# Rounded and low part of x as one moving operand of 512 columns in a hybrid-layer kernel

## Chip, cores and metric

The kernel runs on one core of one Trainium2 chip. The metric is device time in microseconds, the median of several executions. Engines in the profile: PE (TensorE), PEld (its weight loads), DVE (VectorE), ACT (ScalarE), POOL (GpSimd) and SP (the queue that issues most loads).

## The reference, cut to what matters

One layer with four branches over x (256 tokens x 2048 features, fp32), all fed by one wide projection, and merged by gates.

```python
h = einsum('bsd,de->bse', x, w_in) + b_in          # 2048 -> 18048 columns
(a_x, a_gate, q, k, v, b_gate, c_r, c_k, c_v, c_wd, c_ad, c_gate,
 d_val, d_glu, d_gate, merge_logits) = split(h, ...)
y_a = gated linear recurrence over a causal convolution of a_x
y_b = attention of q, k, v in three groups, 4 heads each
y_c = RWKV-7 recurrence over shifted c_r, c_k, c_v, c_wd, c_ad
y_d = silu(layernorm(31-tap depthwise conv(d_val * sigmoid(d_glu))))
merge_g = sigmoid(merge_logits)                    # 4 x 2048 columns
mixed = sum_n merge_g[n] * ((y_n * silu(gate_n)) @ w_br[n])
out = layernorm(ALPHA * x + mixed @ w_out) * ln_g + ln_b
```

## The kernel before

**Precision.** Matmuls of the large products take fp32r operands. Each fp32 operand is split into a rounded part (h) and what is left (l), and a product is three matmuls: h with rounded x, h with low x, l with rounded x. x is split once, by `split_x`, into `xh` and `xl`, each 128 partitions x 16 row blocks x 256 tokens. Weights are split as they arrive: `split` (L202) loads a chunk (two row blocks x 512 columns, 512 KB) to `raw` over SP's queue, ScalarE casts it to `wh` (L208), DVE subtracts to get `wl`. There are four buffers of `raw`, three of `wh`, three of `wl`. DVE's instructions all carry L65, the helper that issues them.

**Two forms of product.** `channel_major` (matmuls in `multiply`, L229) holds weights and moves x: out are 128 channels x 256 tokens per column tile; two tiles share a PSUM bank, so 512 columns take two banks. `token_major` (L279) holds x and moves 512 weight columns; 256 tokens take two banks. Both loop over eight chunks of weights; in channel-major the four column tiles are the loop inside a chunk, then its two row blocks, then the three matmuls. Both take banks from `pss` (four banks). Side work takes banks from `psb` (four).

**Order.** The main stream is: `opening` (a_x and d_glu), d_val, c_r, the 128 columns c_wd and c_ad (`cwa`), c_k, c_v, gate A, merge of A, gate D, merge of D, gate C, queries, keys, values, gate B, merge of C, merge of B, output product, layernorm. After each chunk, `pump(BUD)` lets the generators in `side` (parameter loads, `lru`, `conformer`, `rwkv`, `attention`) issue work worth a budget of 1300 ns; they run one after another. DVE work of `side` keeps its program order. A scheduler then sets a fixed order on each engine from a model of times; the two instructions of a weight split are raised in priority by `AHEAD`.

**Leaving PSUM.** `biased` and `head_tiles` (L887, L936) empty a channel-major plane by one ScalarE instruction (identity with bias). `silu_gate` (L299) uses one ScalarE sigmoid and one DVE instruction that adds the bias to the plane and multiplies.

**Buffers.** `tt` gives planes of 128 x 4 x 256 fp32 out of five, `rk` out of twelve, `ra` 512 columns out of six. `merge` loads a bias row block for each 512 columns over GpSimd's queue into `bm` (two buffers, L842). That queue also carries the recurrent branch's trips through DRAM (`scr`, `al`, `xt`, `x11`). At the end `shift` takes three banks of `psb` for each half of the tokens.

Of the kernel before, what the change touches and what calls it, by code (L numbers as in the profile page):

```python
# [19 lines left out]
P = 128  # L20
# [53 lines left out]
def tile_hybrid(  # L74
# [8 lines left out]
    ap = ctx.enter_context(tc.tile_pool(name="ap", bufs=1))  # L83
    wp = ctx.enter_context(tc.tile_pool(name="wp", bufs=1))
    xp = ctx.enter_context(tc.tile_pool(name="xp", bufs=1))
    bp = ctx.enter_context(tc.tile_pool(name="bp", bufs=1))
    pss = ctx.enter_context(tc.tile_pool(name="pss", bufs=4, space=PSUM))
    psb = ctx.enter_context(tc.tile_pool(name="psb", bufs=4, space=PSUM))
    dp = ctx.enter_context(tc.tile_pool(name="dp", bufs=1, space=DRAM))

    def big(tag, bufs, name, dt=F32):
        pool = ap if tag in ("mx4", "tt") else xp if tag in ("yh", "yl") else bp
        return pool.tile([P, NJ, T], dt, tag=tag, name=name, bufs=bufs)

    def tt(name, dt=F32):
        return big("tt", 5, name, dt)

    def rk(name, dt=F32):
        return big("rk", 12, name, dt)
# [11 lines left out]
    for _ in range(9):  # L111
        PE.matmul(idle, zero[:, 0:P], zero, start=True, stop=True)

    xh = xp.tile([P, KT, T], F32R, tag="xh", name="xh")
    xl = xp.tile([P, KT, T], F32R, tag="xl", name="xl")
    xr = x_t.rearrange("(k p) t -> p k t", p=P)

    def load_x(k, n):
# [10 lines left out]
    sums = cp.tile([P, CS_X0 - CS_BLK], F32R, name="sums")  # L129
    pkt = cp.tile([P, NJ, N_PK], F32, name="pkt")  # L130
    mut = cp.tile([P, 13], F32, name="mut")
    upt = cp.tile([P, BW], F32, name="upt")
    bd = []

    def load(t, src):
        tc.keep_in_program_order(nc.sync.dma_start(t, src))

    def load_parameters():
        for _ in range(5):
            yield pause()  # L140
        load(bc, b_col)
        load(mut, mu)
        yield pause()
        load(pkt, pk)
        yield pause()
        load(upt, w_up)
        yield pause()
        load(cs, cst[:, 0:CS_BLK])
        t = rk("sums_f").rearrange("p a b -> p (a b)")[:, 0 : CS_X0 - CS_BLK]
        load(t, cst[:, CS_BLK:CS_X0])  # L150
        V.tensor_copy(sums, t)
        yield pause()
        blocks = rk("blocks")
        V.memset(blocks, 0.0)
        bd.extend((blocks[:, :, 0:P], blocks[:, :, P:T]))
        for t, src in zip(bd, (gate_a, gate_x)):
            s4 = src.rearrange("(j e) i o -> i j e o", e=2)
            load(t[0:64, :, 0:64], s4[:, :, 0, :])
            load(t[64:128, :, 64:128], s4[:, :, 1, :])
            yield pause()  # L160
# [38 lines left out]
        pump(1e12)  # L199


    def split(src, c0, n, k, nk, queue=None):  # L202
        raw = wp.tile([P, nk, n], F32, tag="raw", name="raw", bufs=4)
        (queue or nc.sync).dma_start(raw, src[:, k : k + nk, c0 : c0 + n])
        h = wp.tile([P, nk, n], F32R, tag="wh", name="wh", bufs=3)
        l = wp.tile([P, nk, n], F32R, tag="wl", name="wl", bufs=3)
        with tc.high_priority(offset=AHEAD):
            S.copy(h, raw)  # L208
            V.tensor_tensor(l, raw, h.bitcast(F32), op=ALU.subtract)
        return h, l  # L210
# [27 lines left out]
    def channel_major(src, nk, c0, n, rh, rl, budget):  # L238
        ps = columns(n)
        for k0, kn in pieces(nk, n):  # L240
            multiply(ps, *split(src, c0, n, k0, kn), k0, kn, nk, rh, rl)
            pump(budget * n * kn / (512 * KP))
        return ps

    def opening(cols, budget):

# [45 lines left out]
        return channel_major(w_in_r, KT, c0, n, xh, xl, BUD)  # L292

    def silu_gate(c0, name):
        ps = proj(c0)
        g = tt(name)
        for j in range(NJ):
            b = bcol(c0 + j * P)
            S.activation(g[:, j, :], ps[j], AF.Sigmoid, bias=b)  # L299
            V.scalar_tensor_tensor(g[:, j, :], ps[j], b, g[:, j, :], op0=ALU.add, op1=ALU.mult)  # L300
        return g

    def gated(y, g, name):
# [34 lines left out]
    def lru(ax, sps, res):  # L338
        (sp8,) = sps
        u = tt("u")  # L340
        for j in range(NJ):
            V.tensor_scalar(u[:, j, :], ax[:, j, :], col(PK_CONV + 3, j), col(PK_CONVB, j), op0=ALU.mult, op1=ALU.add)
            for back in range(1, 4):
                o = u[:, j, back:T]
                V.scalar_tensor_tensor(o, ax[:, j, 0 : T - back], col(PK_CONV + 3 - back, j), o, op0=ALU.mult, op1=ALU.add)
            yield 1300
        th = tt("th")
        gi = tt("gi")
        for j in range(NJ):
            ps = bank("psg")  # L350
            PE.matmul(ps[:, 0:T], bd[0][:, j, :], u[:, j, :], start=True, stop=True)
            PE.matmul(ps[:, T:], bd[1][:, j, :], u[:, j, :], start=False, stop=True, skip_group_check=True)
            S.activation(th[:, j, :], ps[:, 0:T], AF.Sigmoid, bias=col(PK_GAB, j))
            S.activation(gi[:, j, :], ps[:, T:], AF.Sigmoid, bias=col(PK_GXB, j))
            yield 0
        rd = tt("rd")
        rs = tt("rs")
        for j in range(NJ):
            V.tensor_scalar(th[:, j, :], th[:, j, :], sp8[:, j : j + 1], None, op0=ALU.mult)
        yield 800  # L360
        S.activation(rd, th, AF.Exp, scale=-1.0)
        S.activation(th, th, AF.Tanh, scale=0.5)
        V.tensor_scalar(rd, rd, 0.5, 0.5, op0=ALU.mult, op1=ALU.add)
        V.scalar_tensor_tensor(rs, th, 1.0, rd, op0=ALU.add, op1=ALU.mult)
        yield 1700
        V.scalar_tensor_tensor(rd, rs, 2.0, rd, op0=ALU.subtract, op1=ALU.mult)
        yield 1100
        V.tensor_scalar(rs, th, 1e-33, None, op0=ALU.max)
        S.activation(rs, rs, AF.Sqrt)
        V.tensor_tensor(u, gi, u, op=ALU.mult)  # L370
        yield 1700
        V.scalar_tensor_tensor(th, th, 1e17, rs, op0=ALU.mult, op1=ALU.min)
        yield 1100
        V.scalar_tensor_tensor(th, th, -2.0, rd, op0=ALU.mult, op1=ALU.mult)
        yield 1100
        V.tensor_tensor(u, u, th, op=ALU.mult)
        yield 1100
        V.tensor_scalar(rd, rd, -2.0, -1.0, op0=ALU.mult, op1=ALU.add)
        yield 600
        y = gi  # L380
        for j in range(NJ):
            V.tensor_tensor_scan(y[:, j, :], rd[:, j, :], u[:, j, :], 0.0, ALU.mult, ALU.add)
        yield 1400
        res.append(y)
# [13 lines left out]
    def conformer(cu, res):  # L398
# [8 lines left out]
                    )  # L407
                yield 400
        ps = bank("psm")
        total(ps, parts(acc, tt))  # L410
        mean = bp.tile([P, T], F32, tag="s1", name="mean", bufs=4)
        S.activation(mean, ps[:, 0:T], AF.Copy, scale=1.0 / BW)
        V.tensor_tensor(acc, acc, mean[:, None, :].to_broadcast([P, NJ, T]), op=ALU.subtract)
        sq = tt("csq")
        S.activation(sq, acc, AF.Square)
        yield 1100
        ps = bank("psv")
        total(ps, parts(sq, tt))
        rstd = bp.tile([P, T], F32, tag="s1", name="rstd", bufs=4)
        S.activation(rstd, ps[:, 0:T], AF.Sqrt, bias=eps_ln, scale=1.0 / BW)  # L420
        V.reciprocal(rstd, rstd)
# [61 lines left out]
    def rwkv(craw, cwa, res):  # L483
# [18 lines left out]
        yield 700  # L502
        sg = rk("sg")
        a = rk("a")
        for j in range(NJ):
            ps = bank("pswa")
            PE.matmul(ps[:, 0:T], upt[0:64, j * P : (j + 1) * P], wa[0:64], start=True, stop=True)
            S.activation(sg[:, j, :], ps[:, 0:T], AF.Sigmoid, bias=col(PK_W0, j))
            ps = bank("pswa")
            PE.matmul(ps[:, 0:T], upt[64:128, j * P : (j + 1) * P], wa[64:128], start=True, stop=True)  # L510
            S.activation(a[:, j, :], ps[:, 0:T], AF.Sigmoid, bias=col(PK_A0, j))
            yield 0
# [325 lines left out]
    def merge(n, yh, yl, first, last):  # L838
        for c in range(4):
            c0 = C_M + n * DM + c * 512  # L840
            bias = bp.tile([P, 512], F32, tag="bm", name="bm", bufs=2)
            G.dma_start(bias, row(b_row[c0 : c0 + 512]))  # L842
            ps = token_major(w_in_r, KT, c0, *by_token(xh, xl), BUD)
            gs = []
# [3 lines left out]
                S.activation(g, g, AF.Sigmoid)  # L848
                gs.append(g)
            if last and c == 3:  # L850
                mhl.extend(xp.tile([P, KT, T], F32R, tag="x" + q, name="m" + q) for q in "hl")
                side.extend(channels(i) for i in range(3))
            pb = token_major(w_br_r[:, n * NJ : (n + 1) * NJ, :], NJ, c * 512, *by_token(yh, yl), BUD)
            for t in range(2):
# [33 lines left out]
        return t  # L888

    def shifted(c0, name):  # L890
        return biased(rk(name), c0, proj(c0))

    ya, yb, yc, yd = [], [], [], []
    cu = pad_tile("cu")
# [11 lines left out]

    craw = [shifted(C_R, "cr")]
    cwa = bp.tile([P, T], F32, tag="s1", name="cwa", bufs=4)
    ps = proj(C_WA, 128)
    S.activation(cwa, ps[0], AF.Identity, bias=bcol(C_WA))  # L910
    craw += [shifted(C_CK, "ck"), shifted(C_CV, "cv")]
    side.append(rwkv(craw, cwa, yc))

# [16 lines left out]
    def head_tiles(c0, name):  # L930
        r = []
        for g in range(3):
            t = rk(name)
            ps = proj(c0 + g * 512)
            for j in range(NJ):
                S.activation(t[:, j, :], ps[j], AF.Identity, bias=bcol(c0 + g * 512 + j * P))  # L936
            r.append(t)
        return r

    qt = head_tiles(C_Q, "qt")  # L940
# [17 lines left out]
    merge(1, *yhb, False, True)  # L958


    z = [[tt("z").rearrange("p a b -> p (a b)") for _ in range(2)] for _ in range(2)]
    for t in range(2):
        for i in range(2):
            G.dma_start(z[t][i], x[t * P : (t + 1) * P, i * 1024 : (i + 1) * 1024])
# [182 lines left out]
```

## Time and profile before

| | |
|---|---|
| time, median of 3 runs | 1057.73 us (1057.43 to 1058.16) |
| profiled execution, own time | 1057.35 us |
| its span | 1055.6 us |
| granted TensorE clock, mean | 0.995 of full |
| PEld busy | 921.2 us, 87% |
| ACT busy | 497.0 us, 47% |
| DMA queue of SP and ACT | 185.16 MB, 58.9% of 16 engines' span |

The span runs from the first to the last instruction; the table has what the rows below leave out. Busy time of PE counts matmuls whose ends are modelled and which overlap, so it is an upper figure. "idle <- X" names what ended the idle time before an instruction.

### The profile page before, as it was taken

How to read it: one execution, taken by the hardware profiler on the slowest of the kernel's cores; microseconds unless marked ns; L12 is line 12 of the kernel's file. 1: busy time of each engine (PE TensorE's matmuls, PEld its weight loads, DVE VectorE, ACT ScalarE, POOL GpSimd, SP SyncE). 2: the span in 40 equal slices, each digit the busy share in tenths (PEclk: the TensorE clock that was granted, in tenths of full speed). 3: DMA queues.
4: the chain of work that ended last, by engine and by line, in shares of the span. 5: the costliest groups of instructions: out<-in, count | busy, mean ns of one | idle time of the engine just before them, and what ended most of it. 6: DMA issues, size and time to landing. Idle time of an engine off the chain costs nothing.

```text
span 1055.6 us, 16618 instructions
## 1 busy us (share of the span) xinstructions
PE 1042.8 (99%) x6669; PEld 921.2 (87%) x6669; DVE 722.2 (68%) x985; ACT 497.0 (47%) x594; POOL 41.4 (4%) x75
## 2 busy tenths in 40 slices
PE   7999999999999999999999999999999999999997
PEld 6999999887789877899999998898888888888886
DVE  5769988999969996665544444556666565556656
ACT  3365445557734435434544443346565444345341
POOL 0010000000020020000100000000000000000000
PEclk9999999999999999999999999999999999999998
DMA  8885766665686677555866666664556667676662
GB/s 279 247 254 155 204 187 186 189 183 150 186 215 187 199 206 200 182 154 151 288 180 181 182 187 189 194 183 142 170 154 209 209 202 206 207 226 199 193 192 89
DMA packets 108174, 203.11 MB, mean 192 GB/s; under 512 B 8436, under 2 KB 17296, under 8 KB 108096
## 3 DMA queue, kind: packets, MB, share of 16 engines
q1 hardware_dynamic: 102160, 185.16, 58.9%
q0 software_dynamic: 4928, 15.30, 5.0%
q10 hardware_dynamic: 1008, 1.57, 0.4%
q8 instruction: 52, 0.85, 0.3%
q14 instruction: 26, 0.21, 0.1%
HBM read 198.98 MB, written 5.39 MB: 194 GB/s over the span
## 4 chain that ended last, share of the span: by engine, by line
PE 93%; DVE 3%; DMA 2%; issue 1%; ACT 0%; SPq 0%; DVEq 0%; POOL 0%
PE ps L279 50%; PE ps L229 36%; DVE xw L65 1%; DVE wl L65 1%; PE ps L1056 1%; DMA raw<-in_w_in 1%; DMA x<-scr 1%; PE psl L803 1%; DMA xt<-scr 1%; DVE z L65 0%; PE po L827 0%; PE pab L580 0%; PE pm L872 0%; PE py L736 0%; PE pu L699 0%
## 5 line engine op out<-in xcount | busy, mean ns | idle before, releaser
L65 DVE TENSOR_TENSOR wl<-raw,wh 128x1024 fp32r<-128x1024 f32 (+1 forms) x345 | 417.7, 1213 | 275.5 <-ACT wh L208 274.2
L208 ACT CAST wh<-raw 128x1024 fp32r<-128x1024 f32 (+1 forms) x345 | 358.9, 1043 | 470.4 <-PE ps L279 240.7
L229 PE MATMUL ps<-xh,wh 128*128 128x256 f32 x1040 | 295.2, 285 | 4.3 <-ACT wh L208 4.3
L229 PE MATMUL ps<-xl,wh 128*128 128x256 f32 x1040 | 294.1, 284 | 0.0
L229 PE MATMUL ps<-xh,wl 128*128 128x256 f32 x1040 | 291.7, 285 | 0.0
L279 PE MATMUL ps<-wh,xh 128*128 128x512 f32 x608 | 237.9, 391 | 0.0
L279 PE MATMUL ps<-wh,xl 128*128 128x512 f32 x608 | 237.2, 390 | 0.0
L279 PE MATMUL ps<-wl,xh 128*128 128x512 f32 x608 | 221.0, 393 | 0.5 <-DVE wl L65 0.5
L229 PEld LDWEIGHTS ps<-xh,wh 128*128 128x128 f32 x1040 | 199.1, 191 | 5.8 <-ACT wh L208 4.5
L229 PEld LDWEIGHTS ps<-xl,wh 128*128 128x128 f32 x1040 | 199.1, 191 | 0.3
L229 PEld LDWEIGHTS ps<-xh,wl 128*128 128x128 f32 x1040 | 196.9, 191 | 0.7 <-DVE wl L65 0.2
L279 PEld LDWEIGHTS ps<-wl,xh 128*128 128x128 f32 x608 | 114.1, 188 | 26.4 <-DVE wl L65 1.6
L279 PEld LDWEIGHTS ps<-wh,xl 128*128 128x128 f32 x608 | 114.1, 188 | 23.9 <-issue 0.3
L279 PEld LDWEIGHTS ps<-wh,xh 128*128 128x128 f32 x608 | 114.2, 188 | 23.2 <-ACT wh L208 0.3
L65 DVE SCALAR_TENSOR_TENSOR acc<-cu,pkt,acc 128x256 f32<-128x256 f32 x120 | 50.7, 481 | 0.0
L279 PE MATMUL ps<-wh,ml 128*128 128x512 f32 (+1 forms) x128 | 46.5, 364 | 0.0
L279 PE MATMUL ps<-wh,mh 128*128 128x512 f32 (+1 forms) x128 | 46.3, 363 | 0.0
L279 PE MATMUL ps<-wl,mh 128*128 128x512 f32 (+1 forms) x128 | 43.0, 364 | 0.0
L842 POOL DMA_DIRECT2D bm<-in_b_row x16 | 8.8, 551 | 653.1 <-DVE mg L65 625.0
L279 PEld LDWEIGHTS ps<-wh,mh 128*128 128x128 f32 x128 | 24.2, 189 | 3.8
L279 PEld LDWEIGHTS ps<-wh,ml 128*128 128x128 f32 x128 | 24.2, 189 | 3.7
L279 PEld LDWEIGHTS ps<-wl,mh 128*128 128x128 f32 x128 | 24.0, 189 | 3.7
(319 smaller groups left out, 885.5 us busy)
## 6 DMA issues: line engine op xcount, KB each, us to landing
raw<-in_w_in SPq DMA_DIRECT2D x280, 512.0 KB, 4.0
raw<-in_w_br SPq DMA_DIRECT2D x32, 512.0 KB, 4.5
raw<-in_w_out SPq DMA_DIRECT2D x32, 512.0 KB, 4.7
bm<-in_b_row POOLq DMA_DIRECT2D x16, 256.0 KB, 4.3
fscr<-frow POOLq DMA_DIRECT2D x3, 768.0 KB, 7.7
z<-in_x POOLq DMA_DIRECT2D x4, 512.0 KB, 6.6
xs<-in_x_t SPq DMA_DIRECT2D x7, 256.0 KB, 8.1
hb<-fscr POOLq DMA_DIRECT2D x3, 512.0 KB, 4.4
```

What stands on the lines that cost most here:

```text
L65: ins = f(*a, **k)
L208: S.copy(h, raw)
L229: PE.matmul(ps[j], w[:, k, (j - j0) * P : (j - j0 + 1) * P], r[:, kk, :], start=(kk == 0 and i == 0 and j % 2 == 0), stop=(kk == nk - 1 an ...
L279: PE.matmul(ps[t][:, 0:n], a(kk, t), w[:, k, :], start=(kk == 0 and i == 0), stop=(kk == nk - 1 and i == 2),)
L803: PE.matmul(ps[:, 0:w], qt[g][:, h, q * P : (q + 1) * P], kt[g][:, h, 0:w], start=True, stop=True)
L842: G.dma_start(bias, row(b_row[c0 : c0 + 512]))
L1056: PE.matmul(ps[:, 0:T], mix(a)(k, t), w[k // 4][:, k % 4, :], start=(k == 0 and i == 0), stop=(k == KT - 1 and i == 2))
```

## The change

The two parts of x lie side by side in one tile `x2`, token columns of the rounded part followed by those of the low part. A new function `wide` takes the place of the channel-major product in the gates, in c_r, c_k, c_v, cwa, and in queries and keys; `opening` and d_val keep `channel_major`. In `wide` each column tile has a bank of its own, with the product with rounded x in its first half and the product with low x, plus the low weights' product, in its second. `whole` adds the two halves and the bias. Rounded weights of `wide` have a tag of their own (`wa`, three buffers) in a pool that lies above x. To make room, `tt` has three buffers, some planes move to `rk`, the parameter `upt` goes to `ra`, `bm` has one buffer, a quarter of z takes the place of `yh`; `pss` has five banks and `psb` three.

```diff
-    pss = ctx.enter_context(tc.tile_pool(name="pss", bufs=4, space=PSUM))
-    psb = ctx.enter_context(tc.tile_pool(name="psb", bufs=4, space=PSUM))
+    pss = ctx.enter_context(tc.tile_pool(name="pss", bufs=5, space=PSUM))
+    psb = ctx.enter_context(tc.tile_pool(name="psb", bufs=3, space=PSUM))
...
-        return big("tt", 5, name, dt)
+        return big("tt", 3, name, dt)
...
-    xh = xp.tile([P, KT, T], F32R, tag="xh", name="xh")
-    xl = xp.tile([P, KT, T], F32R, tag="xl", name="xl")
+    x2 = xp.tile([P, KT, 2, T], F32R, tag="x2", name="x2")
+    xh, xl = x2[:, :, 0, :], x2[:, :, 1, :]
...
-        h = wp.tile([P, nk, n], F32R, tag="wh", name="wh", bufs=3)
+        h = (wq if above else wp).tile([P, nk, n], F32R, tag="wa" if above else "wh", name="wh", bufs=3)
...
+    def wide(c0, n=512):
+        ps = [pss.tile([P, 512], F32, tag="ps", name="ps") for _ in range(n // P)]
+        for k0, kn in pieces(KT, n):
+            h, l = split(w_in_r, c0, n, k0, kn, above=True)
+            for j in range(n // P):
+                cols = slice(j * P, (j + 1) * P)
+                for k in range(kn):
+                    kk = k0 + k
+                    both = x2[:, kk, :, :].rearrange("p a t -> p (a t)")
+                    PE.matmul(ps[j], h[:, k, cols], both, start=(kk == 0), stop=False, skip_group_check=True)
+                    PE.matmul(
+                        ps[j][:, T:], l[:, k, cols], xh[:, kk, :], start=False, stop=(kk == KT - 1), skip_group_check=True
+                    )
+            pump(BUD * n * kn / (512 * KP))
+        return ps
+
+    def whole(o, ps, b):
+        with tc.high_priority(offset=AHEAD):
+            S.activation(o, ps[:, T:], AF.Identity, bias=b)
+            V.tensor_tensor(o, o, ps[:, 0:T], op=ALU.add)
...
     def silu_gate(c0, name):
-        ps = proj(c0)
+        ps = wide(c0)
         g = tt(name)
         for j in range(NJ):
-            b = bcol(c0 + j * P)
-            S.activation(g[:, j, :], ps[j], AF.Sigmoid, bias=b)
-            V.scalar_tensor_tensor(g[:, j, :], ps[j], b, g[:, j, :], op0=ALU.add, op1=ALU.mult)
+            whole(g[:, j, :], ps[j], bcol(c0 + j * P))
+        for j in range(NJ):
+            s = bp.tile([P, 512], F32, tag="mg", name="sg", bufs=2)[:, 0:T]
+            S.activation(s, g[:, j, :], AF.Sigmoid)
+            V.tensor_tensor(g[:, j, :], g[:, j, :], s, op=ALU.mult)
         return g
...
-            bias = bp.tile([P, 512], F32, tag="bm", name="bm", bufs=2)
+            bias = bp.tile([P, 512], F32, tag="bm", name="bm", bufs=1)
...
     def shifted(c0, name):
-        return biased(rk(name), c0, proj(c0))
+        t = rk(name)
+        for j, ps in enumerate(wide(c0)):
+            whole(t[:, j, :], ps, bcol(c0 + j * P))
+        return t
...
-    ps = proj(C_WA, 128)
-    S.activation(cwa, ps[0], AF.Identity, bias=bcol(C_WA))
+    whole(cwa, wide(C_WA, P)[0], bcol(C_WA))
...
-    z = [[tt("z").rearrange("p a b -> p (a b)") for _ in range(2)] for _ in range(2)]
+    z = [tt("z"), tt("z"), tt("z"), big("yh", 1, "z")]
+    z = [[z[2 * t + i].rearrange("p a b -> p (a b)") for i in range(2)] for t in range(2)]
```

`head_tiles` calls `shifted` for each of its three planes; the merged product's two parts also share a tile with tag `x2`.

## Rows read from the trace of the kernel before

**Rows 1.** The page: busy time and share of engines, granted clock in slices.
```profile
PE 1042.8 (99%) x6669; PEld 921.2 (87%) x6669; DVE 722.2 (68%) x985; ACT 497.0 (47%) x594; POOL 41.4 (4%) x75
PEclk9999999999999999999999999999999999999998
```
**Rows 2.** Waits of PE: line, releaser, us in total, times, longest us.
```profile
PE ps L229 <- ACT wh L208: 4.3, 1, 4.3
PE idle L112 <- DVE zero L65: 1.2, 1, 1.2
PE pp L639 <- DMA x<-scr: 0.8, 1, 0.8
```
**Rows 3.** Chain in order of time: start, us, what, number of instructions.
```profile
75.89 106.55 PE ps L229 x888
...
496.27 129.80 PE ps L229 x1080
...
646.80 45.39 PE ps L279 x200
...
719.54 1.29 PE po L827 x6
```
**Rows 4.** Timeline of PE: start, us, engine, line, operation, tiles, shapes.
```profile
305.73 0.39 PE L279 MATMUL ps<-wl,yah 128*128 128x512 f32 x1
305.96 0.28 PE L229 MATMUL ps<-xh,wh 128*128 128x256 f32 x1
```
**Rows 5.** Groups of instructions by line and shape: busy us, mean ns of one.
```profile
L229 PE MATMUL ps<-xh,wh 128*128 128x256 f32 x1040 | 295.2, 285 | 4.3 <-ACT wh L208 4.3
...
L279 PE MATMUL ps<-wl,xh 128*128 128x512 f32 x608 | 221.0, 393 | 0.5 <-DVE wl L65 0.5
...
L1028 PE MATMUL pn<-rows,lt 2*128 2x512 f32 x8 | 5.0, 753 | 0.7 <-ACT lt L1024 0.7
...
L65 DVE TENSOR_TENSOR sv<-pst,sd 64x256 f32<-64x256 f32 x6 | 2.5, 422 | 1.1 <-PE pst L730 1.0
...
L65 DVE SCALAR_TENSOR_TENSOR ga<-ps,bc,ga 128x256 f32<-128x256 f32 x4 | 1.8, 476 | 0.0
...
L887 ACT ACTIVATE cr<-ps,bc 128x256 f32<-128x256 f32 x4 | 1.7, 469 | 1.0 <-PE ps L229 1.0
```
**Rows 6.** Busy time by stretch: us, then PE, PEld, DVE, ACT, POOL.
```profile
83.00:182.00 99.00, 99.00 (x827) 99.00 (x826) 91.18 (x150) 44.44 (x51) 0.00 (x0) 1.00 0.65 186
182.00:320.00 138.00, 138.00 (x786) 112.97 (x785) 122.68 (x178) 81.53 (x104) 11.49 (x18) 1.00 0.64 185
...
496.00:626.00 130.00, 130.00 (x1084) 129.87 (x1083) 62.72 (x58) 59.07 (x74) 3.91 (x6) 1.00 0.68 206
```
**Rows 7.** Timeline of DVE in c_k's product.
```profile
122.95 1.23 DVE L65 TENSOR_TENSOR wl<-raw,wh 128x1024 fp32r<-128x1024 f32 x1 [0.47 <-ACT wh L208]
124.10 1.67 DVE L65 SCALAR_TENSOR_TENSOR acc<-cu,pkt,acc 128x256 f32<-128x256 f32 x4
```
**Rows 8.** Timeline of DVE and ACT: gate B's product and its cast.
```profile
804.09 1.23 DVE L65 TENSOR_TENSOR gb<-yb,gb 128x1024 f32<-128x1024 f32 x1 [1.41 <-ACT yb L830]
...
844.16 1.05 ACT L307 CAST ybh<-gb 128x1024 fp32r<-128x1024 f32 x1
```
**Rows 9.** Timeline of ACT at the end of c_r's product.
```profile
106.63 0.84 ACT L887 ACTIVATE cr<-ps,bc 128x256 f32<-128x256 f32 x2 [0.98 <-PE ps L229]
```
**Rows 10.** Timeline of POOL's issues around a bias load.
```profile
383.62 0.54 POOL L842 DMA_DIRECT2D bm<-in_b_row  x1 [28.02 <-DVE mg L65]
384.21 0.54 POOL L621 DMA_DIRECT2D scr<-xw  x1
```
**Rows 11.** Timeline of DVE in the tail.
```profile
1048.86 2.71 DVE L65 SCALAR_TENSOR_TENSOR z<-z,rstd,pn 128x512 f32<-128x512 f32 x4
```
**Rows 12.** Timeline of DVE after gate A's product.
```profile
183.28 0.48 DVE L65 SCALAR_TENSOR_TENSOR ga<-ps,bc,ga 128x256 f32<-128x256 f32 x1
...
189.10 0.48 DVE L65 SCALAR_TENSOR_TENSOR ga<-ps,bc,ga 128x256 f32<-128x256 f32 x1
```

More of the change, by code (lines that the diff above doesn't have):

```diff
@@ L85, in tile_hybrid @@
     xp = ctx.enter_context(tc.tile_pool(name="xp", bufs=1))
+    wq = ctx.enter_context(tc.tile_pool(name="wq", bufs=1))
     bp = ctx.enter_context(tc.tile_pool(name="bp", bufs=1))
-    pss = ctx.enter_context(tc.tile_pool(name="pss", bufs=4, space=PSUM))
-    psb = ctx.enter_context(tc.tile_pool(name="psb", bufs=4, space=PSUM))
+    pss = ctx.enter_context(tc.tile_pool(name="pss", bufs=5, space=PSUM))
+    psb = ctx.enter_context(tc.tile_pool(name="psb", bufs=3, space=PSUM))
     dp = ctx.enter_context(tc.tile_pool(name="dp", bufs=1, space=DRAM))
@@ L131, in tile_hybrid @@
     mut = cp.tile([P, 13], F32, name="mut")
-    upt = cp.tile([P, BW], F32, name="upt")
+    ups = []
     bd = []
@@ L145, in load_parameters @@
         yield pause()
-        load(upt, w_up)
+        ups.append(ra("upt", [P, BW]))
+        load(ups[0], w_up)
         yield pause()
@@ L199, in drain, with split @@
         pump(1e12)
-    def split(src, c0, n, k, nk, queue=None):
+    def split(src, c0, n, k, nk, queue=None, above=False):
         raw = wp.tile([P, nk, n], F32, tag="raw", name="raw", bufs=4)
         (queue or nc.sync).dma_start(raw, src[:, k : k + nk, c0 : c0 + n])
-        h = wp.tile([P, nk, n], F32R, tag="wh", name="wh", bufs=3)
+        h = (wq if above else wp).tile([P, nk, n], F32R, tag="wa" if above else "wh", name="wh", bufs=3)
         l = wp.tile([P, nk, n], F32R, tag="wl", name="wl", bufs=3)
@@ L355, in lru @@
             yield 0
-        rd = tt("rd")
-        rs = tt("rs")
+        rd = rk("rd")
+        rs = rk("rs")
         for j in range(NJ):
@@ L409, in conformer @@
         ps = bank("psm")
-        total(ps, parts(acc, tt))
+        total(ps, parts(acc, rk))
         mean = bp.tile([P, T], F32, tag="s1", name="mean", bufs=4)
@@ L413, in conformer @@
         V.tensor_tensor(acc, acc, mean[:, None, :].to_broadcast([P, NJ, T]), op=ALU.subtract)
-        sq = tt("csq")
+        sq = rk("csq")
         S.activation(sq, acc, AF.Square)
@@ L417, in conformer @@
         ps = bank("psv")
-        total(ps, parts(sq, tt))
+        total(ps, parts(sq, rk))
         rstd = bp.tile([P, T], F32, tag="s1", name="rstd", bufs=4)
@@ L504, in rwkv @@
         a = rk("a")
+        (upt,) = ups
         for j in range(NJ):
@@ L850, in merge @@
             if last and c == 3:
-                mhl.extend(xp.tile([P, KT, T], F32R, tag="x" + q, name="m" + q) for q in "hl")
+                m2 = xp.tile([P, KT, 2, T], F32R, tag="x2", name="m2")
+                mhl.extend(m2[:, :, i, :] for i in range(2))
                 side.extend(channels(i) for i in range(3))
@@ L932, in head_tiles @@
         for g in range(3):
[L933 to L937, printed above, removed]
+            r.append(shifted(c0 + g * 512, name))
         return r
```

## The prediction

> **What bounds the kernel now.** I read the page first: the span is 1055.6 us, PE shows 99% busy, DVE 68% [rows 1]. Since ends of matmuls are modelled, a busy PE proves little, so next I read the waits of PE: in all it lost 4.3 us to ScalarE's first cast of weights, 1.2 us to the first memset, 0.8 us to one DMA, and every other releaser less [rows 2]. The reader is to see that between the first weights and the tail nothing holds TensorE up for longer than 0.8 us: its stream of instructions is the time. What remains is what one matmul costs, and for that the chain in order of time is the right view, since it gives long unbroken stretches with counts. The channel-major product with 256 moving columns ran 1080 matmuls in 129.80 us, 120.2 ns each; the token-major one with 512 columns ran 200 in 45.39 us, 227.0 ns each [rows 3]. The clock granted is full, 2.4 GHz [rows 1], so 256 and 512 columns stream in 106.7 and 213.3 ns. Both shapes thus carry 13.5 to 13.7 ns on top: the extra goes with the instruction, not with the columns. Every matmul in both has its own weight load, and single starts show the 512 step keeping its 0.23 us when a 256-column matmul with other weights follows [rows 4]. The durations of single matmuls (285 and 391 ns, [rows 5]) overlap and are not used.
>
> **The change part by part.** 1. *The product.* Per 128-column tile and row block, three matmuls of 256 columns (h with rounded x, h with low x, l with rounded x) become one of 512 (h with both) and one of 256. Streamed columns stay 768; one instruction and one weight load go. Of the 65 column tiles (1040 matmuls of one kind over 16 row blocks, [rows 5]), the opening (8) and C_DV (4) keep the old form by the diff. So 53 change: four gates (16), C_R, C_CK, C_CV (12), C_WA (1), queries and keys (24). That is 53 x 16 = 848 pairs. Each saves 2 x 120.19 - 226.95 = 13.43 ns: **11.4 us**. No reordering by the chip is assumed; a stationary operand of 128 x 128 with 512 contiguous moving columns is the form of the 227 ns row.
>
> Bounds of this term: below, 1.5 us, from plain fp32 rows: six matmuls of 256 columns took 1.29 us [rows 3], 215.0 ns for what is 2 x 106.7 = 213.3 ns at two passes, so only 1.7 ns per instruction; 848 x 1.7 = 1.5 us. Above, 13.7 x 848 = 11.6 us, the 512 row's own extra. I take 11.4, because its two rows are of this operand type and this weight pattern.
>
> The Trainium skill has a rule against this. Its page "TensorE: Matmul & The Clock Gate", section "Wait — 56ns, not 53.3ns?", gives a warm matmul a fixed cost of about 2.5 ns beyond its columns. Estimated by that page the change would save 848 x 2.5 = 2.1 us. The trace does not agree for these matmuls: 120.2 and 227.0 ns where the page would have about 109 and 216.
>
> 2. *Emptying PSUM.* A rounded plane needs bias and sum: ScalarE as before (469 ns, [rows 5]), then a new DVE add from PSUM. The nearest row, an add of 256 columns from PSUM, is 422 ns; the gate's product from PSUM is 476 [rows 5]. 37 such adds (9 tiles of four, and C_WA) make 15.6 us of DVE. A gate's 16 planes go from one DVE instruction (476) to an add and a product (2 x 422), 16 x 0.37 = 5.9 us, and ScalarE gets 16 more, 7.5 us. Together 21.5 us of DVE, were it all on the path; at nothing, if hidden. What hides it: over 496 to 626 us (queries and keys, 24 of the 37 adds) DVE works 62.7 of 130 us, all cover. Over 83 to 182 us (17 changed tiles) it works 91.2 of 99 [rows 6]. There the new need is 91.2 + 13 x 0.42 + 4 x 0.37 = 98.1 us, in 99 - 17 x 16 x 0.01343 = 95.3 us of TensorE: 2.8 us too much. But what fills DVE there are the convolution taps of side work, three or four per chunk of weights [rows 7], and the next stretch has 15.3 us free (122.7 of 138) to take six or seven of them. The weight split runs two chunks ahead (three buffers of h and l; a cast starts when a chunk of three before is used up), so some 3 us of lateness reach nobody. If the taps kept their places, 2.8 us would come back as waits.
>
> Side work that slips has room: the last side chain, attention, gives gb at 804.1 to 805.3 us, and its cast waits for a buffer until 844.2 us [rows 8], some 39 us. So a slower chain, from three side banks of PSUM in place of four as well, costs nothing up to there.
>
> 3. *Banks.* A wide tile takes four of five banks; before it took two of four. The next tile has one bank at once and needs the first plane's bank one block (0.69 us) into itself. That plane ended three blocks before its tile's end, so its emptying has 2.08 + 0.69 = 2.8 us; each further plane has the same. The work in order: wait for a cast in progress (up to 1.05), 0.47 for ScalarE, wait for a weight split (up to 1.15 us a step, [rows 7]), 0.42 for the add: 0.9 to 3.1 us. With four taps (1.67 us) ahead, up to 4.8. There are ten borders between wide tiles: C_R to C_WA to C_CK to C_CV to the first gate (four, DVE full) and gate C_CG through queries to keys (six, DVE half idle). At worst 4 x 2.0 + 6 x 0.3 = 9.8 us; at best 0. ScalarE today empties C_R's planes in pairs, the first within the tile's last chunk [rows 9], and the emptying now has the same raised priority as the weight split, so I take 0.25 us at four borders: **+1.0 us**.
>
> 4. *Buffers.* The merge bias has one buffer: its load for the next column block waits for this block's two bias adds. That load is issued on GpSimd's queue, behind which the recurrent branch's transfers stand (al<-scr, scr<-xw). But the queue already waits for the same adds, with one buffer more of lead: at 383.62 us it issues a bias straight after them and the scratch transfer 0.6 us later [rows 10]. The load has a whole merge block (over 20 us) to land. Nothing; up to 4 us in one place if a scratch transfer is caught behind. z's fourth quarter now waits for yh, free with the last branch product; it is read two column blocks later. Nothing. Three planes tt in place of five, the rk and ra rotations, upt: nothing, the chains are serial and had one or two live at a time beside the gate. Rounded weights of wide tiles in their own three buffers: a switch between forms gains lead, not priced.
>
> 5. *Tail.* With three side banks, the second half's last product needs a bank that the first half's first final pass frees. Those passes run from 1048.86 us, 0.68 each [rows 11]; bank free at 1049.5, product 0.75 us [rows 5] until 1050.3, and it is needed by the fourth pass at 1050.9. Nothing; at worst 0.7 us.
>
> Sum: the profiled execution took 1057.35 us (span 1055.6 and 1.75 around it). 1057.35 - 11.4 + 1.0 = 1046.95. The median of the runs is 0.4 us above that execution, so I say **1047.2 us**, 1.0% less.
>
> **The rivals.** A. *The extra belongs to the operand type, not to the instruction.* Then only 1.5 us go; with 1.0 lost at the borders 1057.2, no change. For it: plain fp32 rows have 1.7 ns. Against: two sizes of the same type give the same extra. By the 2.5 ns of the Trainium skill's page "TensorE: Matmul & The Clock Gate" (section "Wait — 56ns, not 53.3ns?") the estimate would be 1056.6; no row of these matmuls shows such a spacing.
>
> B. *The gain is eaten where DVE is full.* If taps keep their places ahead of the adds, the four early borders wait 2.0 us each and 2.8 us of excess are paid: 1057.7 - 11.4 + 8 + 2.8 = 1057.1, no change. Half of that gives 1051.7. For it: 92% DVE over that stretch. Against: DVE there still has a gap of 0.47 us ahead of a weight split [rows 7] and raised priority for the adds.
>
> C. *Slower: the wide tile's planes are emptied late everywhere.* One mechanism: an add that stands behind side work holds its bank, and TensorE stops in the next tile's second and third block. Its size is seen in today's first gate: its matmuls end at 75.89 + 106.55 = 182.44 us [rows 3], its four DVE passes run from 183.28 to 189.58 [rows 12]. The second, about a third of the way (some 185.4 to 186.4), frees the bank that the next tile's third block wants 1.4 us after the end, so that block would start up to 2.6 us late, 2.7 with the block before it. At all ten borders that is 27 us: 1057.7 - 11.4 + 27 = 1073. It turns slower from 1.35 us per border (11.4 + 2.1 over ten). For it: emptying of a gate did trail by 7 us. Against: that gate had two free banks and no raised priority, so nothing pressed; and six of ten borders stand where DVE is half idle.
>
> **How the numbers follow.** Forecast 0.76, from 1044.8 (11.6 saved and the 1.6 of DMA and small waits gone too) to 1050.5 (11.4 saved, 4 lost at borders or in a queue). B in its half form 0.09 (1051 to 1055, still faster), A and full B 0.07, C 0.08. What a measurement of this kernel can tell from no change is about 0.2%, 2.1 us. Faster 0.85, same 0.07, slower 0.08. The range from 1044.8 to 1053.0 holds the forecast and most of half B; A, C and the rest of B stay out.
>
> **What would show it.** Right: 848 matmuls of 512 columns from h and x2 and 848 of 256 from l, running at about 347 ns a pair in the stretch of queries and keys, which should shrink by 24 x 16 x 13.4 ns = 5.2 us; PE's waits still under a few us, DVE busy some 20 us more. Step 1 is wrong if a pair takes 359 ns or more. Step 3 is wrong if PE waits for DVE or ScalarE at the second to fourth block of a wide tile. Step 4 is wrong if a scratch transfer's issue follows a late bias. The prediction fails if any of these passes 6 us, or if more than 53 tiles changed form.

## The result, and the profile after

| | before | after |
|---|---|---|
| median | 1057.95 us (1057.43 to 1060.08, 4 runs) | 1071.97 us (1070.22 to 1072.59, 4 runs) |
| profiled execution, own time | 1057.35 us | 1072.59 us |
| granted TensorE clock, mean | 0.995 | 0.986 |

The ratio is 1.0131, with a 95% interval of 1.0117 to 1.0145: the changed kernel is slower by 1.3%. The forecast was 1047.2 us, 1.0% faster, and slower had a chance of 0.08. Of all the runs in this document one was slow (in c1, 1280.45 us at a granted clock of 0.75), and the ratios leave it out.

The page of the changed kernel (span, busy time, granted clock in slices, the two groups of the new product):

```profile
span 1070.8 us, 14967 instructions
PE 1044.2 (98%) x5821; PEld 879.3 (82%) x5821; DVE 736.7 (69%) x1038; ACT 500.3 (47%) x608; POOL 41.4 (4%) x75
PEclk9999999999999999997999999999999999999998
L257 PE MATMUL ps<-x,wh 128*128 128x512 f32 x848 | 292.5, 399 | 3.8 <-DVE gc L65 3.8
L258 PE MATMUL ps<-x,wl 128*128 128x256 f32 x848 | 219.0, 283 | 1.3 <-DVE wl L65 1.3
```

The change did what it says: 848 instructions of each form, 848 matmuls fewer on PE than in [rows 1]. What is new stands in the third line, a 7 in the nineteenth slice: near 490 us the clock fell. The waits of PE (line, releaser, us in total, times, longest):

```profile
PE ps L231 <- ACT wh L210: 4.4, 2, 3.8
PE ps L257 <- DVE gc L65: 3.8, 1, 3.8
PE psvar L496 <- DVE selr L65: 2.7, 1, 2.7
PE pst L844 <- DVE lg L65: 2.7, 1, 2.7
PE psvar L480 <- ACT sq L770: 1.5, 1, 1.5
```

Against [rows 2] there are four new entries. The first of them says that the product's stream waited for gate C's sum (`gc`); the others are waits of side work's matmuls, which stand in PE's fixed order with nothing else left to put ahead of them. Two windows show the idle time (columns as in [rows 6], then granted clock, DMA share, GB/s), of before and then of after:

```profile
480.00:500.00 20.00, 20.00 (x160) 17.75 (x159) 11.66 (x16) 8.96 (x10) 0.80 (x1) 1.00 0.52 156
720.00:760.00 40.00, 40.00 (x197) 33.75 (x197) 26.58 (x42) 26.83 (x35) 0.54 (x1) 1.00 0.52 157
```

```profile
83.00:182.00 99.00, 97.68 (x555) 84.39 (x554) 95.94 (x166) 47.13 (x55) 0.00 (x0) 1.00 0.62 179
480.00:500.00 20.00, 12.03 (x126) 7.74 (x124) 9.65 (x17) 7.76 (x14) 2.38 (x4) 0.81 0.25 85
500.00:520.00 20.00, 19.09 (x96) 16.61 (x97) 12.56 (x17) 8.84 (x11) 2.04 (x3) 0.85 0.68 211
501.00:505.50 4.50, 4.50 (x14) 3.83 (x15) 3.50 (x8) 2.25 (x5) 1.31 (x2) 0.50 0.67 218
720.00:760.00 40.00, 36.46 (x176) 30.43 (x175) 24.84 (x40) 21.54 (x31) 0.00 (x0) 0.96 0.46 134
```

PE works 12 of 20 us where it had worked all 20, then runs for a while at half clock (0.50), and near 730 us it works 36.5 of 40. The timeline of the first place, PE, ACT and DVE:

```profile
483.33 0.40 PE L257 MATMUL ps<-x,wh 128*128 128x512 f32 x1
...
488.95 3.48 PE L480 MATMUL psvar<-sq,cs 128*8 128x256 f32 x8 [1.55 <-ACT sq L770]
...
492.84 1.52 ACT L266 ACTIVATE gc<-ps,bc 128x256 f32<-128x256 f32 x4
...
495.17 1.94 PE L496 MATMUL psvar<-selr 8*128 8x256 f32 x8 [2.74 <-DVE selr L65]
...
499.30 1.23 DVE L65 TENSOR_TENSOR yc<-wy,bn 128x1024 f32<-128x1024 f32 x1
500.44 1.40 DVE L65 TENSOR_TENSOR gc<-gc,ps 128x256 f32<-128x256 f32 x4
...
500.91 0.79 PE L257 MATMUL ps<-x,wh 128*128 128x512 f32 x1 [3.80 <-DVE gc L65]
```

From 483.6 us to 500.9 us not one matmul of the large product runs; only the last steps of the recurrent branch do. Gate C's product is done by then, but its four banks are emptied late: on ACT at 492.84 us, right behind the recurrent branch's `sel` (492.47), and on DVE at 500.44, right behind the branch's last output `yc`. The queries get going within 0.5 us of that. The fixed order of PE's instructions in the program has the same gap in it (of the large product the first matmul of a chunk, of side work only the last two steps; tiles with their numbers; `ps_4526` is gate C's last plane, `ps_4730` to `ps_4733` are the first query tile's):

```
L257 MATMUL ps_4526<-x2_93,wh_4683      gate C, last plane
L257 MATMUL ps_4730<-x2_93,wh_4736      queries, plane 0, chunk 0
L257 MATMUL ps_4730<-x2_93,wh_4758      plane 0, chunk 1
L257 MATMUL ps_4730<-x2_93,wh_4780      plane 0, chunk 2
L480 MATMUL psvar_4180<-sq2_4156,cs_95
L496 MATMUL psvar_4225<-selr_4178
L257 MATMUL ps_4731<-x2_93,wh_4736      plane 1, chunk 0
```

Plane 0 takes the one free bank over as many chunks as there are weight buffers, three. Then the product can't go on.

To see where the whole difference lies, the executions are cut in PE's timeline, each stage from its first matmul behind the last one of the stage before (us; what lies ahead of the first product and behind the last is left out):

| | to gate A's end | merge A | gate D | merge D | gate C, queries, keys | values | gate B | merges C, B, output | last columns |
|---|---|---|---|---|---|---|---|---|---|
| before | 178.0 | 123.7 | 23.0 | 120.7 | 176.2 | 66.1 | 25.3 | 316.2 | 10.6 |
| after | 178.2 | 124.7 | 23.9 | 117.8 | 188.1 | 65.8 | 23.3 | 322.4 | 10.6 |
| e1 | 176.3 | 124.7 | 24.1 | 118.0 | 174.1 | 65.8 | 23.3 | 322.5 | 10.6 |
| e4 | 177.2 | 124.7 | 23.8 | 116.7 | 174.1 | 65.8 | 23.3 | 317.0 | 10.6 |

Of +15.0 us, 11.9 are in the stretch that begins with gate C and 6.2 in the one behind gate B; everything else together gains 3.1.

### The profile page after: what moved, and what is told of

Its sections match the earlier page's. It is cut to its first block, busy times and chain, and to the rows that moved or that the text cites. A ratio compares the mean times of both kernels' runs of the same rounds, so it can differ in the third digit from the quotient of the medians.

```text
span 1070.8 us, 14967 instructions
## 1 busy us (share of the span) xinstructions
PE 1044.2 (98%) x5821; PEld 879.3 (82%) x5821; DVE 736.7 (69%) x1038; ACT 500.3 (47%) x608; POOL 41.4 (4%) x75
## 4 chain that ended last, share of the span: by engine, by line
PE 86%; DVE 7%; DMA 2%; issue 2%; ACT 1%; POOL 0%; SPq 0%; DVEq 0%
PE ps L303 48%; PE ps L257 17%; PE ps L258 9%; PE ps L231 5%; DVE wl L65 2%; DMA raw<-in_w_in 2%; DVE xw L65 1%; PE ps L1083 1%; PE psl L830 1%; DMA x<-scr 1%; PE po L854 0%; ACT wh L210 0%; DVE z L65 0%; DVE d L65 0%; POOL xt L657 0%
## 5 line engine op out<-in xcount | busy, mean ns | idle before, releaser
L303 PE MATMUL ps<-wh,x 128*128 128x512 f32 x1216 | 360.6, 391 | 1.8 <-ACT wh L210 0.9
L257 PE MATMUL ps<-x,wh 128*128 128x512 f32 x848 | 292.5, 399 | 3.8 <-DVE gc L65 3.8
L303 PEld LDWEIGHTS ps<-wh,x 128*128 128x128 f32 x1216 | 227.8, 188 | 49.7 <-ACT wh L210 1.3
L303 PE MATMUL ps<-wl,x 128*128 128x512 f32 x608 | 222.5, 394 | 0.9 <-DVE wl L65 0.9
L258 PE MATMUL ps<-x,wl 128*128 128x256 f32 x848 | 219.0, 283 | 1.3 <-DVE wl L65 1.3
L257 PEld LDWEIGHTS ps<-x,wh 128*128 128x128 f32 x848 | 156.9, 189 | 34.3 <-DVE gc L65 4.1
L258 PEld LDWEIGHTS ps<-x,wl 128*128 128x128 f32 x848 | 161.1, 190 | 11.0 <-DVE wl L65 2.5
L303 PEld LDWEIGHTS ps<-wl,x 128*128 128x128 f32 x608 | 114.1, 188 | 27.1 <-DVE wl L65 3.1
L231 PE MATMUL ps<-x,wh 128*128 128x256 f32 x384 | 70.9, 289 | 4.4 <-ACT wh L210 4.4
L303 PE MATMUL ps<-wh,m 128*128 128x512 f32 (+1 forms) x256 | 67.9, 364 | 0.0
L231 PEld LDWEIGHTS ps<-x,wh 128*128 128x128 f32 x384 | 60.6, 196 | 5.1 <-ACT wh L210 4.8
L231 PE MATMUL ps<-x,wl 128*128 128x256 f32 x192 | 53.2, 286 | 0.0
L231 PEld LDWEIGHTS ps<-x,wl 128*128 128x128 f32 x192 | 36.5, 194 | 0.2 <-DVE wl L65 0.2
```

Of the source, the lines that this page charges most:

```text
L231: PE.matmul(ps[j], w[:, k, (j - j0) * P : (j - j0 + 1) * P], r[:, kk, :], start=(kk == 0 and i == 0 and j % 2 == 0), stop=(kk == nk - 1 an ...
L257: PE.matmul(ps[j], h[:, k, cols], both, start=(kk == 0), stop=False, skip_group_check=True)
L258: PE.matmul(ps[j][:, T:], l[:, k, cols], xh[:, kk, :], start=False, stop=(kk == KT - 1), skip_group_check=True)
L303: PE.matmul(ps[t][:, 0:n], a(kk, t), w[:, k, :], start=(kk == 0 and i == 0), stop=(kk == nk - 1 and i == 2),)
```

## The experiments

Theory 1: planes of one tag are handed out in program order. `yc = tt("yc")` stands before gate C's `g = tt("gc")`, and attention's `y = tt("yb")` before gate B's; so no gate can be emptied until the older plane has been given its turn, and a wide gate holds four of five banks meanwhile. The rivals: the smaller buffers (three planes `tt`, one `bm`, three side banks), the place of the rounded weights above x, and rival C of the prediction, late emptying at all ten borders.

**e1_yc_in_place** takes `yc` out of the tag, on the changed kernel:

```diff
-        yc = tt("yc")
-        V.tensor_tensor(yc, wy, bn, op=ALU.add)
+        V.tensor_tensor(wy, wy, bn, op=ALU.add)
...
-        res.append(yc)
+        res.append(wy)
```

> The changed kernel with one edit: the recurrent branch's last sum is written over wy, so that it takes no plane of tt. Theory 1 (planes in program order): gate C's plane of tt is handed out only after yc's, so its four banks stay full until the recurrence has ended, and queries have one bank; with the edit the stretch from gate C through the keys shrinks from 188.1 us to about 172 (176.2 before, less 28 x 16 pairs at 10 ns), and the whole from 1072 to about 1056 us. Rival (fewer side banks and one bias buffer slow the recurrence): no such return, 1069 to 1073 us, and PE still idle before the queries.

Measured: 1057.06 us beside 1057.38 of before, ratio 0.999 (0.9977 to 1.0003). Nearly 15 us of the loss went with one plane. DVE's timeline of e1, and its window:

```profile
476.43 1.07 DVE L65 TENSOR_TENSOR gc<-gc,ps 128x256 f32<-128x256 f32 x3
...
505.33 1.73 DVE L65 RECIPROCAL sel<-sel 8x256 f32<-8x256 f32 x1
```

```profile
480.00:500.00 20.00, 20.00 (x189) 17.00 (x188) 9.87 (x15) 9.16 (x13) 1.57 (x3) 1.00 0.57 166
700.00:760.00 60.00, 56.44 (x276) 47.41 (x275) 36.92 (x57) 33.29 (x46) 0.55 (x1) 0.97 0.50 149
```

The gate is emptied at 476 us, while the recurrent branch's end (the reciprocal `sel`) comes later than in the changed kernel, at 505 in place of 493, and holds nothing up: PE is full. The stretch from gate C through the keys takes 174.1 us, where about 172 had been expected. The second hole, near 730 us, is still there.

**c1_before_yc** makes the same edit in the kernel before, as a control.

> The kernel before with the same edit as the first run (the recurrent branch's last sum over wy). Theory 1: no change, 1057 to 1059 us, because there gate C holds two banks of four and queries have the other two. Rival (the edit is a gain of its own, whatever the banks): several us faster than before.

Measured: 1057.13 beside 1057.38, ratio 0.9994 (0.9982 to 1.0006): nothing. The kernel before had the same order of planes, as DVE's timeline of before shows, but its gate held two banks of four and the queries went on in the other two:

```profile
499.71 1.23 DVE L65 TENSOR_TENSOR yc<-wy,bn 128x1024 f32<-128x1024 f32 x1
...
502.14 0.88 DVE L65 SCALAR_TENSOR_TENSOR gc<-ps,bc,gc 128x256 f32<-128x256 f32 x2
```

**e2_buffers** keeps the change's buffers and banks (only the tag `wa` falls out of use), and goes back to the old product and emptying (cut here: the same for `silu_gate`'s emptying and `cwa`):

```diff
     def silu_gate(c0, name):
-        ps = wide(c0)
+        ps = proj(c0)
...
-        for j, ps in enumerate(wide(c0)):
-            whole(t[:, j, :], ps, bcol(c0 + j * P))
-        return t
+        return biased(rk(name), c0, proj(c0))
```

> The changed kernel's buffers (five and three banks, three planes of tt, one bias buffer, x side by side) with the old products and the old emptying. Theory 1: the buffers alone cost little, because gate C then holds two banks of five: within 2 us of 1057.9. Rival (buffers): 1064 us or more.

Measured: 1058.37 beside 1057.38, ratio 1.0002 (0.9991 to 1.0013). Fewer planes, one `bm` and three side banks cost nothing by themselves.

**e3_below** puts the rounded weights of `wide` back below x:

```diff
-        h = (wq if above else wp).tile([P, nk, n], F32R, tag="wa" if above else "wh", name="wh", bufs=3)
+        h = wp.tile([P, nk, n], F32R, tag="wa" if above else "wh", name="wh", bufs=3)
```

> The changed kernel with the rounded weights of wide tiles in the pool below x, nothing else. A chunk of eight pairs takes 2.805 us in the queries' stretch with the weights above x, where 2.777 was reckoned. If the place doesn't matter: 2.80 to 2.81 us again and 1070 to 1073 us in all. If weights below x are slower for the 512-column matmul: over 2.85 us a chunk and over 1075 us; if they are faster, 2.78 us and 1068 to 1070 us.

Measured: 1069.88 beside 1057.38, ratio 1.011 (1.0095 to 1.0125). The total lies in the band named for faster weights, but a group of four column tiles takes 22.50 us of the queries' stretch, 2.81 a chunk, just as in the changed kernel: the place of the weights isn't the cause. The wait for `gc` is there as in the changed kernel, as e3's waits of PE show:

```profile
PE ps L257 <- DVE gc L65: 3.8, 1, 3.8
```

**e4_both** adds to e1 the same for gate B, **e5_yb_only** does that alone:

```diff
-        y = tt("yb")
+        y = pad_tile("yb")[:, :, 0:T]
```

> The first run's edit and, for attention, its output yb in the tile of the convolution's input (long dead) in place of a plane of tt. Theory 1: gate B's four banks are held behind yb as gate C's were behind yc, and the 6.3 us that the stretch after gate B still lost in the first run (322.5 us against 316.2) come back: 1050 to 1052 us, clearly faster than before. Rival (sigmoid and exponential tables changing places on ScalarE stop TensorE there, or three side banks do): 1056 to 1058 us again.

> The changed kernel with only yb moved out of tt, yc as it was. Theory 1: the two holds add up, so only the second goes: 1065 to 1067 us, and the stretch from gate C through the keys stays at 187 to 188 us. Rival (one common cause, such as the side banks): nothing or all of it changes.

Measured: e4 1051.21 (1050.28 to 1053.3) beside 1056.58 of before, ratio 0.9942 (0.9929 to 0.9956); e5 1065.51, ratio 1.0073 (1.005 to 1.0095). So by the medians the second hold costs 5.9 us with the first one gone and 6.5 with it in place (5.1 and 6.1 by the ratios to before): the two add up. In e5 the stretch from gate C through the keys takes 186.4 us, a little under the 187 to 188 expected. In the changed kernel (ACT and PE) and then in e4 (ACT and DVE) gate B's emptying stands so to `yb`:

```profile
733.41 0.37 ACT L857 COPY yb<-po 128x256 f32<-128x256 f32 x1 [2.96 <-PE po L856]
733.68 1.57 ACT L266 ACTIVATE gb<-ps,bc 128x256 f32<-128x256 f32 x4
...
734.67 0.73 PE L303 MATMUL ps<-wh,x 128*128 128x512 f32 x2 [0.84 <-DVE gb L65]
```

```profile
708.53 0.87 ACT L266 ACTIVATE gb<-ps,bc 128x256 f32<-128x256 f32 x2
709.40 1.14 DVE L65 TENSOR_TENSOR gb<-gb,ps 128x256 f32<-128x256 f32 x3
...
720.69 0.37 ACT L856 COPY yb<-po 128x256 f32<-128x256 f32 x1 [2.95 <-PE po L855]
```

The order is reversed: ACT's four instructions, which had stood right behind attention's first output, now begin 12 us ahead of it. PE of e4 is full there:

```profile
700.00:760.00 60.00, 60.00 (x297) 50.71 (x296) 37.97 (x53) 32.81 (x43) 0.54 (x1) 1.00 0.59 173
```

e4 beats both kernels: it is the change without its two holds.

**e6_gc_apart** leaves `yc` alone and takes the gate's plane from another pool; **e9_five_planes** gives `tt` its five planes back (room comes from letting wide tiles share the three `wh` buffers), and keeps the order:

```diff
-        g = tt(name)
+        g = pad_tile(name)[:, :, 0:T] if name == "gc" else tt(name)
```

```diff
-        return big("tt", 3, name, dt)
+        return big("tt", 5, name, dt)
...
-        h = (wq if above else wp).tile([P, nk, n], F32R, tag="wa" if above else "wh", name="wh", bufs=3)
+        h = wp.tile([P, nk, n], F32R, tag="wh", name="wh", bufs=3)
```

> The changed kernel with gate C's own plane taken from the convolution's dead input tile, while yc keeps its plane of tt. Theory 1 (the gate waits for its plane because planes of a tag are handed out in program order): as the first run, 1055 to 1058 us, with the stretch from gate C through the keys near 174 us. Rival (the first run was quicker because the recurrence lost an output to allot, not because of the gate's plane): 1069 to 1073 us.

> The changed kernel with five planes of tt as before; the room comes from the rounded weights of wide tiles, which share the three buffers of the others. Theory 1 (order, not number): no return, 1068 to 1073 us, gate C's banks still emptied after yc. Rival (three planes are too few): 1055 to 1060 us.

Measured, beside 1056.58: e6 1057.07, ratio 1.0001 (0.999 to 1.0011); e9 1072.05, ratio 1.0136 (1.012 to 1.0152). This pair separates order from number. Two more planes change nothing: from gate C's first matmul to the first of values e9 takes 185.8 us, as the changed kernel does. One plane outside the row takes the first hold away, from the gate's side as well as from `yc`'s: e6 needs 174.1 us from gate C through the keys, as e1 does.

**e7_budget** asks whether e4 loses time early because DVE is full: side work is issued at a lower rate, on top of e4.

```diff
-            pump(BUD * n * kn / (512 * KP))
+            pump(1000.0 * n * kn / (512 * KP))
```

> The run with both planes moved, and the side work's budget in a chunk of wide tiles lowered from 1300 to 1000. Theory (in the 17 early wide tiles DVE is what runs out, as step 2 reckoned 2.8 us of excess): that stretch, 177.2 us to the end of gate A, falls by 1 to 3 us, the taps go to the merge behind it, and the whole comes to 1048 to 1050.5 us. Rival (the early loss isn't DVE's): 1051 us or more, side work only later.

Measured: 1050.84 beside 1057.17, ratio 0.994 (0.9927 to 0.9954), not to be told from e4. The first stretch shrank by only 0.9 us (177.2 to 176.3); side work then lay later (gate D 23.8 to 28.7, gate C with queries and keys 174.1 to 176.6, the merges of A and D together 241.4 to 234.0). Inconclusive: the changed kernel, e1, e4, e5 and e6 have the same instructions in the same order up to gate A's end, and their single executions take from 175.8 to 178.2 us there, so 0.9 us tells nothing. The budget moves the load about and doesn't show what the full DVE costs.

**e8_qk_only** uses the wide form for queries and keys alone (24 column tiles), with e4's planes.

```diff
     def silu_gate(c0, name):
-        ps = wide(c0)
+        ps = proj(c0)
...
+    def plain(c0, name):
+        return biased(rk(name), c0, proj(c0))
...
-    craw = [shifted(C_R, "cr")]
+    craw = [plain(C_R, "cr")]
```

> The run with both planes moved, but the wide form in queries and keys alone; gates, c_r, c_k, c_v and cwa by the old product and the old emptying. Theory: six groups of four column tiles at 0.54 to 0.71 us each, as the casts of the queries' stretch show, and nothing lost where DVE is full: 1053 to 1054.5 us, 3 to 4 less than before. Rival (the wide form pays only through the other tiles): 1056 us or more.

Measured: 1053.84 beside 1057.17, ratio 0.9965 (0.9954 to 0.9977), 3.3 us less. Queries and keys give more than half of e4's gain with less than half of the tiles.

**e10_grouped** puts, within a column tile of e4, both 512-column matmuls first and then both of 256: same instructions, another order.

```diff
+                for k in range(kn):
+                    kk = k0 + k
                     PE.matmul(
```

> The run with both planes moved, and within a column tile's two row blocks first the two matmuls of 512 columns, then the two of 256. If the extra of a matmul hangs on what follows it (a weight load hidden under 256 or under 512 columns), a tile of eight chunks in the queries' stretch changes from 22.4 us by 0.3 us or more; if it goes with the instruction, it stays at 22.3 to 22.5 us and the whole at 1050 to 1052 us.

Measured: 1056.83 beside 1057.17, ratio 0.9991 (0.9981 to 1.0001). In the queries a group of four column tiles took 22.30 us where e4 takes 22.33, so the order inside a tile made no difference there. The total missed what was expected: the whole fixed order came out otherwise, and the time went elsewhere, as a window of e10 and its waits of PE show:

```profile
330.00:450.00 120.00, 115.38 (x647) 93.07 (x647) 101.23 (x149) 55.88 (x71) 9.81 (x17) 0.99 0.65 189
```

```profile
PE ps L305 <- DVE wl L65: 5.1, 5, 2.6
```

In the merges PE waited 5.1 us for weight splits on DVE. Why the new order puts them there was not followed up.

## Why the prediction was wrong, point by point

**Step 4 failed, and with it step 3 at two of its borders.** Step 4 put the three planes of `tt` in place of five at "nothing, the chains are serial and had one or two live at a time beside the gate". It counted how many planes are alive, and three are indeed enough (e4 runs with three, and the five of e9 change nothing). What it left out is when a plane is handed out: a gate's plane comes after `yc` (gate C) and after `yb` (gate B), although its product is ready earlier. Step 3 then gave gate C's border to the queries 0 to 0.3 us, "where DVE is half idle", and didn't count gate B's border to the merge at all, since that is no border between wide tiles. The runs show 14.0 us of stretch (188.1 to 174.1) and 14.9 us of median (1071.97 to 1057.06) at the first, 5 to 6.5 us at the second. Step 3's own sign of being wrong, PE waiting for DVE at the second block of a wide tile, is the wait of 3.80 us for `gc` at 500.91 us.

The hold lies in the fixed order: ACT's pass over gate C came at 492.84 us, before `yc` was written (499.30 us), but right behind `sel`, its own engine's last step towards `yc`, and DVE's pass came behind `yc` itself. The first hold can be followed further. PE is idle 8.0 us between 480 and 500 us and 0.9 in the next 20. The granted clock is 0.50 from 501.0 to 505.5 us, 1.2 GHz in place of 2.4, and was low before that too, 0.53 over 489.0 to 492.4 us: there the sums of squares (`psvar` L480) take 3.48 us where e1's timeline has 1.89, and eight pairs from 500.91 to 506.04 us take 5.13 in place of 2.81. That makes 8.9 + 1.6 + 2.3 = 12.8 of the 14.0 us; the rest was not followed up.

Both late emptyings could be read from the trace of before: DVE's pass for gate C ran at 502.14 us, right behind `yc` and some 18 us after its product, whose matmuls end near 484 us; likewise gate B's ACT pass came behind `yb`:

```profile
721.54 0.37 ACT L830 COPY yb<-po 128x256 f32<-128x256 f32 x1 [3.06 <-PE po L829]
...
723.21 0.84 ACT L299 ACTIVATE gb<-ps,bc 128x256 f32<-128x256 f32 x2
```

A late emptying of two banks cost nothing then, because the other two were free.

**Rival C** named the right mechanism, held banks, at the wrong place: ten borders at 2.7 us each, from work ahead in DVE's order. In fact no border between wide tiles but the one after gate C shows as a wait of its own in PE's list, and e1 to e5 put the loss at two places of some 15 and 6 us. That its 1073 us lies next to the 1071.97 measured is chance.

**Step 1 was right in kind and too large.** ACT's casts, one per chunk, give the pace in the queries; two casts a whole group of four column tiles (64 pairs of a tile and a row block) apart, of before, of after and of e4:

```profile
548.23 1.05 ACT L208 CAST wh<-raw 128x1024 fp32r<-128x1024 f32 x1 [1.83 <-PE ps L229]
...
571.26 1.05 ACT L208 CAST wh<-raw 128x1024 fp32r<-128x1024 f32 x1 [1.83 <-PE ps L229]
```

```profile
543.36 1.05 ACT L210 CAST wh<-raw 128x1024 fp32r<-128x1024 f32 x1 [1.78 <-PE ps L257]
...
565.86 1.05 ACT L210 CAST wh<-raw 128x1024 fp32r<-128x1024 f32 x1 [1.78 <-PE ps L257]
```

```profile
544.46 1.05 ACT L210 CAST wh<-raw 128x1024 fp32r<-128x1024 f32 x1 [1.76 <-PE ps L257]
547.23 1.05 ACT L210 CAST wh<-raw 128x1024 fp32r<-128x1024 f32 x1 [1.72 <-PE ps L257]
550.00 1.05 ACT L210 CAST wh<-raw 128x1024 fp32r<-128x1024 f32 x1 [1.72 <-PE ps L257]
...
572.33 1.05 ACT L210 CAST wh<-raw 128x1024 fp32r<-128x1024 f32 x1 [1.72 <-PE ps L257]
```

A group takes 23.03, 22.50 and (in e4 from 550.00 us) 22.33 us, for each of the 64 pairs 360, 352 and 349 ns. The pair saves 8 to 11 ns, not 13.4; over 848 pairs that makes 7.0 to 9.3 us, an estimate from this stretch, not 11.4. Some chunks of e4 do run at 2.77 us for eight pairs, 346 ns, the forecast's 347; most take 2.80 to 2.83. What is too slow is the 512-column matmul: by the starts in e4's PE timeline, 515 to 610 us, the next one starts 234 ns behind it on average, where the forecast had taken 227 from the token-major product, and 116 ns behind a 256-column one, less than the 120 of before. Why is open: e3 has the same pace with the weights below x, and e10 with the pairs regrouped.

**Rival A fell.** The extra goes with the instruction, since taking one of three away removes most of it. The Trainium skill's page "TensorE: Matmul & The Clock Gate", section "Wait — 56ns, not 53.3ns?", gives a warm matmul about 2.5 ns beyond its columns; by that estimate the pair would save 2.5 ns. The trace does not agree: 8 to 11. What spoke for this rival was misread, too: the six matmuls of plain fp32 in 1.29 us are six records of three instructions (one for each of three groups in `attention`), so that one takes 430 ns, about four times the 106.7 of its 256 columns and 3.3 beyond them. The lower bound would have been 2.8 us, not 1.5, which would not have changed the forecast.

**Step 5 held, and step 2 reckoned too much.** DVE is 14.5 us busier (722.2 to 736.7), where step 2 had 21.5; gate C's four adds took 1.40 us, 0.35 each, where 0.42 had been priced. The last columns take 10.6 us as before. **Rival B** is partly there: DVE works 95.9 of 99 us between 83 and 182 us, and up to the end of gate A the table has -0.2 to 1.7 us saved (after, e4, e1; a spread between single executions, as the instructions are the same there), where 17 tiles at 13.4 ns would give 3.7. How much of that is the full DVE and how much the smaller saving per pair, e7 did not settle. These two terms are the likely reasons why e4 gains 5 to 6 us (0.58% by its ratio) and not the 10.5 of the forecast; what each takes of it is not shown. The ends of the forecast's own range, from the terms that it names, add up to 1044.5 and 1050.3 us and not 1044.8 and 1050.5; nothing hangs on that.

## What to carry to other kernels

A tile that holds more PSUM makes the moment of its emptying count: before widening it, look in the trace of before at when each product's banks are read, not only at whether PE waited for it, since free banks hide a late reader. Where the reader writes into a buffer from a rotating tag, the older requests for that tag in program order are part of its wait. In this kernel more buffers didn't help; a plane of its own, or writing in place, did. Some 10 ns on each of 848 pairs were lost to a single hole of 15 us, so price the holes first.

## What the runs showed of the hardware

Pairs of one 512-column and one 256-column fp32r matmul, each with its own weights, run at 349 to 352 ns, three of 256 columns at 360. In the changed kernel PE idled for most of the time from 487.5 to 489.0, from 492.4 to 495.2 and from 497.0 to 500.9 us, and the matmuls behind these pauses ran at a low granted clock: the sums of squares at 0.53 and the new product at 0.50 (1.2 GHz) until 505.5 us. That cost 1.6 us on the sums of squares and 2.3 us on the new product, on top of the idle time itself.
